# A two-layer hybrid attention block: five moves in the order of issue

## The chip, the core and the metric

The kernel runs on one core of one Trainium2 chip. The metric is the device time of one execution in microseconds, lower is better. A core has a matrix engine (TensorE, PE in the profile, with its weight loads as PEld), a vector engine (VectorE, DVE), an activation engine (ScalarE, ACT), a general engine (GpSimd, POOL) and a queue engine (SyncE, SP), which here issues nearly all DMAs. Each engine works its own list of instructions from first to last. TensorE's clock has two levels, 1.2 and 2.4 GHz; the profile calls the share that was granted PEclk, 1.00 for the higher.

## The reference

Two layers over 256 latent tokens and 256 context tokens of width 1024. Each layer computes, for both kinds of tokens (context only as far as the latents need it in the second layer):

```python
mod = silu_c @ lp["w_mod"] + lp["b_mod"]            # six vectors of 1024: shift, scale, gate, twice
h = modulate(x, lp["g_norm1"], sh1, sc1)            # RMSNorm, then scale and shift
proj = h @ lp["w_in"]
o_mla = blocked_attend(q_mla, k_mla, v_mla, MLA_QK ** -0.5)     # 8 heads
o_gqa = blocked_attend(q_gqa, k_gqa, v_gqa, GQA_DIM ** -0.5)    # 8 heads over 2 key heads
o_four = fourier_mix(proj[..., FOUR_START:GATE_START])          # 2-D DFT over 4 groups of 128 channels
y = (g_mla * (o_mla @ lp["w_br_mla"]) + g_gqa * (o_gqa @ lp["w_br_gqa"])
     + g_four * (o_four @ lp["w_four"]))            # g_* = sigmoid of gate columns of proj
x = x + gt1 * (y @ lp["w_o"])
u = conv3(modulate(x, lp["g_norm2"], sh2, sc2) @ lp["w_up"])
x = x + gt2 * ((silu(u[:D_FF]) * u[D_FF:]) @ lp["w_down"])      # D_FF = 2816
```

All of it is in float32.

## The kernel before

**Precision and weights.** Every large product is made of three matmuls of a reduced float32 type: each operand is split into a high part (a copy on ACT) and a low part (a subtraction on DVE), by `split` (L115), and `mm3` (L103) issues high by high (L104), high by low (L105) and low by high (L106). `wchunk` (L80) loads a chunk of a weight matrix in pieces of 1024 columns' worth (512 KB each, on SP), and splits each piece. The raw pieces, their high and their low parts have three buffers each (`RAWBUFS`, `WBUFS`).

**Who sets the order.** The program is traced in the order of the Python code. Tile then makes each engine's list with a simulated timeline: of the instructions that are ready in the simulation, the one traced earliest goes first, so a later piece of code can be drawn into a hole. `tc.issue_after(ins)` adds an edge: what a block traces on the engine of `ins` stands behind `ins` in that engine's list. It is no wait at run time. `after(mark)` (L111) does the same with an instruction noted in `marks`. `last_mm[0]` is the latest traced matmul of `mm3`.

**A layer** (`layer`, L445) works 512 tokens in layer 0 and 256 latent tokens (with 512 for keys and values) in layer 1. In order: the norm; keys and values of GQA (`kvg`, L500); GQA's queries in two chunks of 256 columns (`qg`, L519); the Fourier branch (`fo`, L596, with the DFT as matmuls from L610); GQA's heads, between which `fillers` put gate and branch products; then `latents`, `kv_tokens` and `q_tokens`, which make MLA's keys and queries; MLA's eight heads, after each of which an entry of `plan` (L897) is traced; the last branch; the output projection with `w_o` (L966 on); the second norm; the feed-forward.

**Gates and branches.** `merge` (L556) gives a gate function (`gG` for GQA, `gM` for MLA: 8 k x 2 x 3 = 48 matmuls and a tanh) and a branch function (`bG`, `bM`: 4 k x 2 x 3 = 24 matmuls, then a multiply on DVE and an addition into y on POOL). Their matmuls have 512 columns in layer 0 and 256 in layer 1.

**MLA's first heads.** `heads_kq(h)` (L905) transposes the keys and the queries of head h on TensorE and splits them. Head 0's is traced right behind `bG(0)`. The key tokens end with a multiply on POOL (L785), the query tokens with a rope on POOL (L495 to L498).

**The output projection.** Four chunks of 256 columns; each runs k = 0 to 7 over `ys`, the split y. The last two of the y come from the last branch product.

**Layer 1's start.** The last down projection of layer 0 ends in two halves of 256 tokens, and layer 1's norm of the latent half (`seq(0)`) is traced between them. The norm of the context half (`seq(1)`) is traced at the start of layer 1; `kvg` then takes the two latent token tiles first and the two context tiles after them.

**The sums.** The modulation vectors of layer 1 are made during layer 0's feed-forward. `mod_sums` (L277) makes, for each of five blocks of 1024 columns, eight steps: a load of 512 KB of `w_mod`, and one or two multiply-adds over it on DVE (L291 for the first k, L293 for the others); the eighth step ends with matmuls (L300), a copy and two transposes. `sums(n)` (L987) traces the next n steps: one behind each pair of columns j of the up projection, four behind the loads of each group of the down projection. The feed-forward runs in two halves of 12 and 10 of the 22 column blocks; a down group is one of four chunks of `w_down` over all k of its half.

## Time and profile before

| | before |
|---|---|
| median of 3 runs | 1407.85 us (1403.91 to 1409.02) |
| the profiled execution | 1404.45 us |
| its span, first to last instruction | 1402.7 us |
| TensorE busy | 1348.4 us (96%) |
| DVE busy | 945.7 us (67%) |
| ACT busy | 660.3 us (47%) |
| POOL busy | 337.5 us (24%) |
| mean granted TensorE clock | 0.982 |
| DMA moved | 197.40 MB, mean 141 GB/s |

The chain of work that ended last lies on TensorE for 86% of the span and on DVE for 7%. Busy times of matmuls overlap, since matmuls are pipelined, so the rate of TensorE is read from counts: instructions in a window of known length. A window's idle time is its length less the busy time.

### The profile page before, as it was taken

What the parts mean: (1) busy time and instruction counts of PE and PEld (TensorE: products, weight loads), DVE (VectorE), ACT (ScalarE), POOL (GpSimd) and SP (SyncE); (2) the same over time, 40 slices, a digit from 0 to 9 for tenths busy, and PEclk for the clock granted to TensorE, in tenths of its full rate; (3) what the DMA queues carried; (4) which work ended last, traced back from release to release, by engine and by line L of the source; (5) the groups of instructions that cost most, each with busy time, mean ns of one, the idle gap of its engine ahead of it and who ended that gap; (6) DMA issues with size and microseconds to landing.
All of it is one profiled execution on the core that took longest, in us unless ns stands there. A gap on an engine that the chain in (4) does not pass through costs nothing.

```text
span 1402.7 us, 22232 instructions
## 1 busy us (share of the span) xinstructions
PE 1348.4 (96%) x8381; PEld 1177.3 (84%) x8381; DVE 945.7 (67%) x1686; ACT 660.3 (47%) x1166; POOL 337.5 (24%) x399
## 2 busy tenths in 40 slices
PE   7999999999999997999999999999997999899998
PEld 4988888878888786887888888888987998899998
DVE  4575665666655669998635664578787766788853
ACT  4444554435554333444223443355664764566642
POOL 3212332374323411111100112122244432112200
PEclk9999999999999998999999999999998999999999
DMA  9733442143321736577632423354423345465663
GB/s 322 243 90 105 151 143 79 54 123 106 90 66 43 268 124 186 162 231 233 201 108 81 126 85 102 103 154 120 125 81 102 106 129 191 134 182 181 182 196 118
DMA packets 160437, 197.40 MB, mean 141 GB/s; under 512 B 7080, under 2 KB 144858, under 8 KB 160330
## 3 DMA queue, kind: packets, MB, share of 16 engines
q1 hardware_dynamic: 159328, 195.32, 45.2%
q0 software_dynamic: 864, 0.61, 0.4%
q8 instruction: 66, 1.08, 0.3%
q14 instruction: 41, 0.34, 0.1%
q10 hardware_dynamic: 138, 0.04, 0.0%
HBM read 191.76 MB, written 3.15 MB: 139 GB/s over the span
## 4 chain that ended last, share of the span: by engine, by line
PE 86%; DVE 7%; DMA 2%; issue 2%; POOL 1%; ACT 1%; SPq 0%; DVEq 0%; ACTq 0%; POOLq 0%
PE L0upp L106 5%; PE L0upp L104 5%; PE L0upp L105 5%; PE L1upp L104 3%; PE L1upp L105 3%; PE L1upp L106 3%; PE L0gp L106 3%; PE L0dp L104 3%; PE L0gp L105 3%; PE L0dp L105 3%; PE L0dp L106 3%; PE L0gp L104 3%; PE L1dp L106 1%; PE L1dp L105 1%; PE L1dp L104 1%
## 5 line engine op out<-in xcount | busy, mean ns | idle before, releaser
L105 PE MATMUL L0upp<-L0n_h,L0up_h 128*128 128x512 f32 (+1 forms) x384 | 144.8, 380 | 4.0 <-POOL L0n_h L373 2.4
L104 PE MATMUL L0upp<-L0n_h,L0up_h 128*128 128x512 f32 (+1 forms) x384 | 144.2, 379 | 2.6 <-ACT L0n_h L370 1.1
L106 PE MATMUL L0upp<-L0n_h,L0up_l 128*128 128x512 f32 (+1 forms) x384 | 142.7, 379 | 0.3 <-DVE L0up_l L124 0.3
L1031 POOL TENSOR_TENSOR L0sg<-L0sg,L0u 128x512 f32<-128x512 f32 x22 | 34.5, 1571 | 275.6 <-DVE L0u L1008 255.6
L104 PE MATMUL L1upp<-L1n_h,L1up_h 128*128 128x256 f32 x352 | 96.9, 287 | 1.1 <-ACT L1n_h L370 1.1
L106 PE MATMUL L1upp<-L1n_h,L1up_l 128*128 128x256 f32 x352 | 96.8, 285 | 0.0
L105 PE MATMUL L1upp<-L1n_h,L1up_h 128*128 128x256 f32 x352 | 96.3, 285 | 0.0
L105 PEld LDWEIGHTS L0upp<-L0n_h,L0up_h 128*128 128x128 f32 x384 | 74.0, 193 | 17.8 <-POOL L0n_h L373 2.6
L104 PEld LDWEIGHTS L0upp<-L0n_h,L0up_h 128*128 128x128 f32 x384 | 73.6, 193 | 16.5 <-ACT L0n_h L370 1.5
L106 PEld LDWEIGHTS L0upp<-L0n_h,L0up_l 128*128 128x128 f32 x384 | 73.7, 192 | 14.8 <-DVE L0up_l L124 1.1
L118 ACT CAST L0up_h<-L0up_w 128x1024 fp32r<-128x1024 f32 x44 | 46.4, 1054 | 76.3 <-PE L0upp L105 51.6
L124 DVE TENSOR_TENSOR L0up_l<-L0up_w,L0up_h 128x1024 fp32r<-128x1024 f32 x44 | 55.9, 1269 | 32.6 <-ACT L0up_h L118 32.3
L293 DVE SCALAR_TENSOR_TENSOR mod_acc<-mod_w,cpad,mod_acc 128x1024 f32<-128x1024 f32 x49 | 70.6, 1456 | 9.5 <-DMA mod_w<-in_w_mod_dram 9.5
L104 PE MATMUL L0gp<-L0n_h,L0g_h 128*128 128x512 f32 x192 | 76.6, 400 | 0.0
L105 PE MATMUL L0gp<-L0n_h,L0g_h 128*128 128x512 f32 x192 | 76.2, 397 | 0.0
L106 PE MATMUL L0gp<-L0n_h,L0g_l 128*128 128x512 f32 x192 | 75.7, 400 | 0.0
L104 PE MATMUL L0dp<-L0act,L0dn_h 128*128 128x512 f32 (+1 forms) x196 | 72.2, 368 | 0.0
L106 PE MATMUL L0dp<-L0act,L0dn_l 128*128 128x512 f32 (+1 forms) x196 | 72.1, 368 | 0.0
L105 PE MATMUL L0dp<-L0act,L0dn_h 128*128 128x512 f32 (+1 forms) x196 | 72.1, 368 | 0.0
L104 PEld LDWEIGHTS L1upp<-L1n_h,L1up_h 128*128 128x128 f32 x352 | 67.1, 195 | 1.8 <-ACT L1n_h L370 1.8
L106 PEld LDWEIGHTS L1upp<-L1n_h,L1up_l 128*128 128x128 f32 x352 | 67.2, 194 | 0.0
L124 DVE TENSOR_TENSOR L1up_l<-L1up_w,L1up_h 128x1024 fp32r<-128x1024 f32 x44 | 54.2, 1232 | 18.9 <-ACT L1up_h L118 17.5
(1564 smaller groups left out, 4279.2 us busy)
## 6 DMA issues: line engine op xcount, KB each, us to landing
mod_w<-in_w_mod_dram SPq DMA_DIRECT2D x96, 512.0 KB, 4.6
L0up_w<-in_w_up_dram SPq DMA_DIRECT2D x44, 512.0 KB, 3.6
L1up_w<-in_w_up_dram SPq DMA_DIRECT2D x44, 512.0 KB, 4.4
L0g_w<-in_w_in_dram SPq DMA_DIRECT2D x24, 512.0 KB, 3.7
L1g_w<-in_w_in_dram SPq DMA_DIRECT2D x24, 512.0 KB, 3.7
L0dn_w<-in_w_down_dram SPq DMA_DIRECT2D x20, 512.0 KB, 3.9
L1dn_w<-in_w_down_dram SPq DMA_DIRECT2D x16, 512.0 KB, 3.6
L0wo_w<-in_w_o_dram SPq DMA_DIRECT2D x8, 512.0 KB, 7.4
```

Source lines behind the costliest of these rows:

```text
L104: nc.tensor.matmul(ps, lh, rh, start=start, stop=False)
L105: nc.tensor.matmul(ps, lh, rl, start=False, stop=False)
L106: last_mm[0] = nc.tensor.matmul(ps, ll, rh, start=False, stop=stop).ins
L118: nc.scalar.copy(hi, src)
L124: nc.vector.tensor_sub(lo, src, f(hi))
L293: nc.vector.scalar_tensor_tensor(acc, raw, cv, acc, op0=ALU.mult, op1=ALU.add)
L1031: nc.gpsimd.tensor_mul(g[:, :TQ], g[:, :TQ], us[1][:, :TQ])
```

## The change

Five edits, all in the order of issue or the place of buffers; what is computed is the same.

- `sums`: each step is now traced under `after("split")` and `after("load")`, so its multiply-adds stand on DVE behind the latest traced low part of a split, and its load on SP behind the latest traced weight load. The eighth step gives back its closing matmuls as `add_up`; they wait in `late` for the next call of `sums`, which traces them behind the last matmul. A call `sums(0)` stands ahead of layer 1's first norm.
- Output projection: chunks 0 and 1 are loaded together; k = 0 to 5 of both run, then k = 6, 7 of both. Chunks 2 and 3 are as before.
- Layer 1's start: the first query chunk is traced between `kvg` of the latent tiles and `kvg` of the context tiles, with split tiles of its own (B0, B1, B2, D0) and in the `pt` banks.
- MLA: gate 1 (layer 0) or 2 (layer 1) of GQA is traced ahead of head 0's transposes, and these stand behind its last matmul on TensorE. In `plan` the gate is left out; in layer 1 the later entries move up by one and the last is empty.
- DFT: the loop over the four groups is outside the loop over the sequences.

In the diff below, the old places of the `kvg` loop and of its evacuation are left out; the loop itself is the one that stands there behind `q_chunk`.

```diff
-    def wchunk(W, k0, nk, c0, ncol, name):
+    def wchunk(W, k0, nk, c0, ncol, name, own=None):
...
-            hi = wpool.tile([P, WMAX], F32R, tag="whi", name=f"{name}_h{i}", bufs=WBUFS)
-            lo = wpool.tile([P, WMAX], F32R, tag="wlo", name=f"{name}_l{i}", bufs=WBUFS)
+            if own:
+                hi, lo = (S.tile([P, WMAX], F32R, tag=t, name=f"{name}_{x}{i}") for x, t in zip("hl", own[len(parts)]))
+            else:
+                hi = wpool.tile([P, WMAX], F32R, tag="whi", name=f"{name}_h{i}", bufs=WBUFS)
+                lo = wpool.tile([P, WMAX], F32R, tag="wlo", name=f"{name}_l{i}", bufs=WBUFS)
             split(raw[:, :n], hi[:, :n], lo[:, :n])
...
-        w.last = ins.ins
+        w.last = marks["load"] = ins.ins
...
         def low():
             if scale is None:
-                nc.vector.tensor_sub(lo, src, f(hi))
+                ins = nc.vector.tensor_sub(lo, src, f(hi))
             else:
-                nc.vector.scalar_tensor_tensor(lo, src, scale, f(hi), op0=ALU.mult, op1=ALU.subtract)
+                ins = nc.vector.scalar_tensor_tensor(lo, src, scale, f(hi), op0=ALU.mult, op1=ALU.subtract)
+            marks["split"] = ins.ins
...
-            if k < KD - 1:
-                return
+            return add_up if k == KD - 1 else None
+
+        def add_up():
             ps = pm(f"{name}_ps{blk}", "tk")
...
+        def q_chunk(c, banks, own=None):
+            w = wchunk(w_in, 0, KD, 928 + c * 256, 256, f"{n_}qg{c}", own)
             marks[f"qg{c}"] = w.last
             for tt in range(NTQ):
                 ts = slice(tt * P, (tt + 1) * P)
-                ps = pm(f"{n_}qg{tt}{c}", ("mm", "s")[tt % 2])
+                ps = pm(f"{n_}qg{tt}{c}", banks[tt % 2])
...
+        for tts in ((0, 1), (2, 3)) if l else (range(4),):
+            for k in range(KD):
+                wh, wl = w3(k, 0, 288)
...
+                        mm3(pss[tt][:, :288], hs[k][:, 0, ts], hs[k][:, 1, ts], wh, wl, k == 0, k == KD - 1)
+            if l and tts[0] == 0:
+                q_chunk(0, ("pt", "pt"), [("B0", "B1"), ("B2", "D0")])
...
+        for c in range(1 if l else 0, 2):
+            q_chunk(c, ("mm", "s"))
...
-        for s in range(NS):
-            for g in range(4):
+        for g in range(4):
+            for s in range(NS):
                 b, hf = (g, s) if NS == 2 else divmod(g, 2)
...
         if last:
-            plan = [[(bG, 1)], [(gG, 2)], [(bG, 2)], [(gG, 3)], [(bG, 3)], [(gM, 0)], [(gM, 1)], [(gM, 2)], [(gM, 3, "D4")]]
+            plan = [[(bG, 1)], [(bG, 2)], [(gG, 3)], [(bG, 3)], [(gM, 0)], [(gM, 1)], [(gM, 2)], [(gM, 3, "D4")], []]
         else:
-            plan = [[(gG, 1), (bG, 1)], [(gG, 2), (bG, 2)], [(gG, 3), (bG, 3)], [],
+            plan = [[(bG, 1)], [(gG, 2), (bG, 2)], [(gG, 3), (bG, 3)], [],
                     [(gM, 1, "X3")], [(gM, 2, "mraw")], [(gM, 3, "mraw")], [], [(gM, 0)]]
...
-        kq = heads_kq(0)
+        gG(2 if last else 1)
+        with tc.issue_after(last_mm[0]):
+            kq = heads_kq(0)
...
-        for mc in range(4):
+
+        wos, pos = [], []
+        for mc in range(2):
+            wos.append(wchunk(a["w_o"][l], 0, KD, mc * 256, 256, f"{n_}wo{mc}"))
+            pos.append([pm(f"{n_}o{mc}_{i}", ("mm", "s")[mc]) for i in range(2)])
+        for ks in (range(6), range(6, KD)):
+            for mc in range(2):
+                for k in ks:
+                    for i in range(2):
+                        wh, wl = wos[mc](k, i * P, P)
+                        mm3(pos[mc][i][:, :TQ], wh, wl, ys[k][:, 0, :TQ], ys[k][:, 1, :TQ], k == 0, k == KD - 1)
+                if ks[-1] == KD - 1:
+                    for i in range(2):
+                        residual(mc * 2 + i, pos[mc][i][:, :TQ], 16)
+        for mc in range(2, 4):
...
         def sums(n):
-            for step in mods["v"][:n]:
-                step()
+
+
+            todo, late[:] = late[:], []
+            for r in todo:
+                with tc.issue_after(last_mm[0]):
+                    r()
+            with after("split"), after("load"):
+                late.extend(r for r in [step() for step in mods["v"][:n]] if r)
             del mods["v"][:n]
+        late = []
...
                 elif mc == 3 and j0:
                     fm_halves(w, [0, P], jn, acts, lambda i, s_, ps: residual_half(mc * 2 + i, s_, ps, 40), f"{n_}dp{j0}{mc}",
-                              lambda: nxt.append(next_norm(xn)))
+                              lambda: (sums(0), nxt.append(next_norm(xn))))
```

## Rows read from the trace of the kernel before

**Rows 1.** The page, part 1: busy us, share of the span, instructions.

```profile
PE 1348.4 (96%) x8381; PEld 1177.3 (84%) x8381; DVE 945.7 (67%) x1686; ACT 660.3 (47%) x1166; POOL 337.5 (24%) x399
```

**Rows 2.** Windows at full stream: length, busy (count) by engine, PEclk, DMA share, GB/s.

```profile
700.00:725.00 25.00, 25.00 (x112) 20.71 (x111) 8.03 (x12) 5.13 (x5) 0.00 (x0) 1.00 0.34 106
...
1250.00:1275.00 25.00, 25.00 (x210) 25.00 (x210) 21.52 (x35) 16.38 (x26) 5.01 (x4) 1.00 0.60 182
```

**Rows 3.** Windows over the places that the edits name, same columns.

```profile
92.00:110.00 18.00, 15.39 (x94) 13.65 (x93) 12.91 (x24) 9.98 (x23) 1.59 (x2) 0.91 0.17 55
276.00:306.00 30.00, 26.95 (x124) 21.70 (x123) 25.49 (x39) 10.36 (x15) 20.36 (x17) 1.00 0.37 106
452.00:464.00 12.00, 8.83 (x39) 6.66 (x38) 12.00 (x13) 6.65 (x10) 10.20 (x6) 1.00 0.55 185
...
526.00:562.00 36.00, 27.65 (x168) 24.04 (x167) 34.41 (x45) 12.39 (x19) 5.43 (x3) 0.81 0.63 188
...
902.00:922.00 20.00, 16.96 (x112) 13.01 (x105) 17.11 (x55) 11.37 (x29) 3.26 (x5) 0.83 0.42 126
...
1068.00:1082.00 14.00, 7.91 (x35) 6.03 (x34) 6.51 (x12) 3.86 (x9) 5.19 (x8) 0.64 0.25 76
1140.00:1156.00 16.00, 16.00 (x135) 15.92 (x133) 9.27 (x14) 9.09 (x16) 3.19 (x5) 1.00 0.51 155
1163.00:1181.00 18.00, 14.59 (x103) 13.43 (x102) 14.12 (x21) 8.03 (x15) 5.14 (x3) 0.91 0.41 130
```

**Rows 4.** Waits of TensorE: who, for whom, us in total, times, longest.

```profile
PE L1kvg L104 <- ACT L1n_h L370: 2.9, 2, 1.8
PE mod_ps L300 <- DVE mod_acc L293: 2.8, 2, 2.3
...
PE L0m0tk L909 <- POOL L0ktok L785: 2.0, 3, 0.9
PE L0o L105 <- DVE L0yh L126: 2.0, 1, 2.0
```

**Rows 5.** Timeline of DVE, head of layer 0's feed-forward: start, us, what.

```profile
526.78 2.47 DVE L293 SCALAR_TENSOR_TENSOR mod_acc<-mod_w,cpad,mod_acc 128x1024 f32<-128x1024 f32 x2
529.17 0.48 DVE L369 SCALAR_TENSOR_TENSOR L0n_t<-L0x,L0A,L0n_rb 128x256 f32<-128x256 f32 x1
```

**Rows 6.** The line L293: durations min/median/max, first and last; its waits.

```profile
L293 DVE SCALAR_TENSOR_TENSOR mod_acc<-mod_w,cpad,mod_acc x49: 1268/1279/2311, 526.8 to 687.8; 128x1024 f32<-128x1024 f32 x49
...
  DMA mod_w<-in_w_mod_dram: 9.5, 7
```

**Rows 7.** Groups on DVE, 700 to 750 us: count, busy us, mean ns, idle before.

```profile
L956 DVE SCALAR_TENSOR_TENSOR L0x<-L0dp,modT,L0x 128x256 f32<-128x256 f32 x12 | 5.0, 478 | 8.0 <-PE L0dp L106 8.0
L124 DVE TENSOR_TENSOR L0dn_l<-L0dn_w,L0dn_h 128x1024 fp32r<-128x1024 f32 x4 | 4.9, 1220 | 8.4 <-ACT L0dn_h L118 8.4
```

**Rows 8.** Timeline of ACT, end of layer 0's DFT.

```profile
102.40 0.58 ACT L836 CAST L0KG<-L0gk 64x512 fp32r<-64x512 f32 x1
...
104.78 0.17 ACT L633 COPY L0z<-L0Zc 128x4 f32<-128x4 f32 x1
```

**Rows 9.** Timeline of POOL, head of MLA in layer 1.

```profile
1071.50 1.10 POOL L495 TENSOR_TENSOR L1qmr0b<-L1qtok,Bqm 128x128 f32<-128x128 f32 x1 [10.42 <-DVE L1qtok L814]
...
1074.58 0.46 POOL L495 TENSOR_TENSOR L1qmr1b<-L1qtok,Bqm 128x128 f32<-128x128 f32 x1
...
1076.21 0.72 POOL L498 TENSOR_TENSOR L1qtok<-L1qmr1a,L1qmr1b 128x256 f32<-128x256 f32 x1
```

**Rows 10.** Timeline of ACT, start of layer 1.

```profile
911.98 0.73 ACT L1124 CAST dft1d<-dft1r 128x256 fp32r<-128x256 f32 x2 [1.96 <-DMA dft1r<-in_dft_d_dram]
```

**Rows 11.** Timeline of DVE, start of layer 0's output projection.

```profile
456.64 4.43 DVE L124 TENSOR_TENSOR L0wo_l<-L0wo_w,L0wo_h 128x1024 fp32r<-128x1024 f32 x2
```

**Rows 12.** The DMA view: issues by tile, KB each, median us to landing.

```profile
mod_w<-in_w_mod_dram SPq DMA_DIRECT2D x96, 512.0 KB, 4.6
...
L0qg_w<-in_w_in_dram SPq DMA_DIRECT2D x4, 512.0 KB, 8.9
```

32 lines of the change are left out of this document (13 added, 19 removed).

## The prediction

> **What bounds the kernel now.** I read the page's busy table first: TensorE is busy 1348.4 of 1402.7 us, DVE 945.7 [rows 1]. So only two things can shorten the run: TensorE's idle time, 54 us, and stretches in which its clock stood at the lower of its two levels. Undisturbed, the stream takes 25/112 = 0.223 us for a matmul of 512 columns and 25/210 = 0.119 us for one of 256 [rows 2]; no edit touches that work. Next I cut the span into the places that the edits name, and read for each the idle time (length minus PE busy) and the lost clock (length times one minus PEclk) [rows 3]: the DFT of layer 0, 2.6 idle and 1.6 lost to the clock; head of MLA in layer 0, 3.05 and 0; start of the output projection of layer 0, 3.2 and 0; head of the feed-forward of layer 0, 8.35 and 6.8; start of layer 1, 3.0 and 3.4; head of MLA in layer 1, 6.1 and 5.0; output projection of layer 1, 3.4 and 1.6. Together 29.7 + 18.4 = 48.1 us. That is a ceiling: some of the slow clock lies on idle time and is counted twice. All else in the sum is how much of each place the edit reaches. Then the waits of TensorE tell who is late there [rows 4].
>
> **Part 1, the sums (L283 to L311, issued from `sums`).** In the head of the feed-forward the multiply-adds of layer 1's modulation sit between the steps of the norm: pairs of 2.47 us, each ahead of a norm step of 0.48 on DVE's queue, with TensorE waiting for the norm [rows 5]; then TensorE itself waits in `mod_ps` for the accumulator, 2.8 us in 2 waits [rows 4]. The 40 steps hold 56 sums (two rows in the first two blocks of eight steps, one in the other three); the 49 that accumulate ran from 527 to 688 us [rows 6]. The change puts each step behind the latest split on DVE and its load behind the latest weight load on SP, and the closing matmuls one call later behind the last matmul traced. So none can stand before the first two columns' splits: 12 sums fall to the first half's six column pairs, 26 to its four down groups, 5 to the second half's pairs, 13 to its down groups. The head loses its cause. The idle is 8.35; with all the clock it would be 15.2, but the two overlap in part. I take 11 gained, ends 6 and 14: the norm's own steps and weight splits may leave a short wait.
>
> What they cost where they go: a down group of layer 0's first half is 12 x 2 x 3 = 72 matmuls, 72 x 0.223 = 16.1 us. DVE has there 3 splits of 1.22 and 4 residuals of 0.48, 5.6 us [rows 7]; the heaviest groups add 8 sums of 1.28 [rows 6], 10.2. That is 15.8 of 16.1. It fits, barely, for two groups of four; the whole half needs 33 + 22 = 55 of 64 us. Queued behind each sum are the next group's weight splits, and behind a sum's load on SP the next weight loads. I take 1 us lost, ends 0 and 10.
>
> **Part 2, DFT by group.** TensorE waits for ACT's copy of the second bank's z, which stands behind four key copies of 0.58 on ACT's queue [rows 8]. With the group loop outside, the first bank is complete after a quarter of the 48 small matmuls instead of five eighths, so the splits and z run some 2 us earlier; but the first group now needs the fourth token tile at once. Ceiling 4.2; I take 3, ends 4.2 gained and 1 lost (that tile's split late). Layer 1 has one s, its order stays.
>
> **Part 3, a gate ahead of MLA's first transposes.** The gate's matmuls move forward and the transposes are put behind them on TensorE. In layer 0 it waits 2.0 us in three waits for POOL's keys [rows 4]; with 48 x 0.223 = 10.7 us of gate ahead these vanish. Queued behind the transposes are head 0's scores, for which only its own softmax waits; the gate's two loads on SP now pass the next branch's, which is used later. I take 2 of 3.05, ends 3 gained and 1 lost. In layer 1 the gate gives 48 x 0.119 = 5.7 us of cover for a place with 6.1 idle and 5.0 of clock. The last wait there is for POOL's rope, which ended at 1076.9 [rows 9]; the gate adds two weight splits to DVE's queue ahead of that chain, 2 x 1.22 by the same shape of [rows 7], so I take 6, ends 11 gained and 1 lost. One pair of rows bears on the lower end: the first rope step took POOL 1.10 us, the same step of the next tile 0.46 [rows 9]. The Trainium skill ("SBUF — State Buffer", section "SBUF: two separate sides") says that a DVE operation with two SBUF inputs and a GpSimd one lock each other out for a whole instruction, as splits of weights would do to the rope. The rows agree with it; if three of the eight rope steps met a split, that would be 3 x 0.64 = 1.9 us later, and by that rule the gain would be nearer 4 than 6.
>
> The gate is taken from the plan of the heads, whose last entry in layer 1 becomes empty: the last head has one gate behind it instead of two. TensorE was busy all 16 us of that stretch [rows 3], and 5.7 us of it go. I take 1 lost, ends 0 and 4, since the last head's own chain is not all covered by what is left.
>
> **Part 4, first queries between keys.** At layer 1's start TensorE waits twice: 2.9 us in all, the longest 1.8 [rows 4]: for a norm step on ACT that stood behind a copy waiting 1.96 for the DFT table's DMA [rows 10], and for the first step of the context half. The chunk's 48 x 0.119 = 5.7 us cover the second wait and let the clock stay up; the first stands ahead of the chunk. Its own tiles let its splits run early, but 2 x 1.22 us more of DVE then compete with the norm, and its two banks are shared with the modulation bursts. On SP its loads pass nothing new: they already stood first after those of `kvg`, and the DFT table's follow them as before. Ceiling 6.4; I take 4, ends 6.4 gained and 1 lost.
>
> **Part 5, output projection in pairs.** It holds back k = 6, 7 of two chunks. But in layer 0 the wait is for the first yh low half, standing behind two weight splits of 4.43 us [rows 4, 11]; it is the only wait of `L0o` for a yh, and it is not at k = 6. So I take 1 for both layers, ends 8 gained (the whole of both places, order falling well) and 2 lost (four parts in three weight buffers).
>
> **Sum**: 11 - 1 + 3 + 2 + 6 - 1 + 4 + 1 = 25 us gained. The profiled execution took 1404.45 us; 25 less is 1379.5. The median of three runs is 3.4 above it, so on that scale 1407.85 - 25 = 1382.9, say 1383. All good ends together give 14 + 0 + 4.2 + 3 + 11 + 0 + 6.4 + 8 = 46.6, all bad ones 6 - 10 - 1 - 1 - 1 - 4 - 1 - 2 = -14; they will not fall together.
>
> **Rivals.** A: the chains, not the cover, set both heads. The extra splits push the rope chain of layer 1 back and the tail loses its gate; then only the sums and the DFT count, 11 - 1 + 3 = 13: 1395. For it: the rope chain ends the last wait, and one of its steps was already stretched to 1.10 us [rows 9]. Against: DVE was idle for half of that stretch, 6.5 of 14 us busy [rows 3], so it has room for two splits.
>
> B, the slower side: the down groups wait for the sums' loads. Two load buffers and four steps a group give a step (load + sums)/2. At the median 4.6 us [rows 12] it is (4.6 + 2.56)/2 = 3.6, 14.3 a group: under 16.1. At 8.9, what a 512 KB load took where loads crowd [rows 12], it is 5.7, 22.9 a group: 6.8 over in four groups; the second half, 60 matmuls and 13.4 us a group, one sum of 1.28 a step, has 20.4, 7.0 over in three. That is 48 lost, 1383 + 48 = 1431. It decides against the change from about 7.2 us a load, where 4 x (2 x (7.2 + 2.56) - 16.1) + 3 x (2 x (7.2 + 1.28) - 13.4) = 24 us are lost, about all that the edits gain. For it: sums already waited 9.5 us for loads [rows 6]. Against: DMA moved 106 GB/s in that stretch [rows 2], the sums add 16 x 0.52 MB in 64 us, 131 more, and the median load is two thirds of the breaking point.
>
> C: the edits hardly show, since the instruction order comes from a simulated schedule that need not place the work as the text suggests, and new waits appear as the old ones go: 1407 give or take 6.
>
> **Chances.** Forecast 0.61 (1360 to 1392), A 0.17, C 0.12, B 0.10. A difference under 0.5% (7 us) can't be told from none in this kernel. Faster by over 0.5% means below 1400.8: forecast and A, 0.78; the same, C, 0.12; slower, B, 0.10. The range 1367 to 1406 holds most of the forecast, A and half of C: about 0.81.
>
> **What would show it.** Part 1: no L293 before 550 us, the head's PE busy near its length at clock 1.00, sums spread to the end of layer 0; wrong if PE goes idle in the down groups. Part 2: no wait in L0Zc. Part 3: no wait for L1m2tk, `gp` ahead of L1m0tk, and TensorE full behind the last head. Part 4: `L1qg` between the two `L1kvg` runs. Part 5: little. I am wrong if the idle leaves these places but the span does not shrink by it.

## The result, and the profile after

The changed kernel took 1387.35 us, the median of four runs (1384.54 to 1390.6), against 1408.43 (1403.91 to 1409.15) for the kernel before on the same chip: ratio 0.9858, 95% interval 0.9827 to 0.9889. So it is faster by 21 us, 1.4%, beyond the 0.5% that this kernel can resolve; 1383 was forecast, within 1367 to 1406. The profiled execution took 1388.23 us with a span of 1386.4.

The page of the changed kernel, part 1 (busy us, share of the span, instructions) and the clock line of part 2 (tenths of full clock in 40 slices):

```profile
PE 1339.8 (97%) x8381; PEld 1171.6 (85%) x8381; DVE 949.8 (69%) x1686; ACT 660.7 (48%) x1166; POOL 334.4 (24%) x399
...
PEclk8999999999999999999999999999999999999999
```

Beside [rows 1]: the instruction counts are the same, and the other engines are as busy as before, to 1%. TensorE's busy time fell by 8.6 us, because at the higher clock the same matmuls are shorter (its mean granted clock rose from 0.982 to 0.988, and 0.006 of the span is 8.3 us); the rest of the 16.3 us of span is idle time that went.

The places of [rows 3] again, moved along with the work: length, busy us of PE, PEld, DVE, ACT and POOL (count), PEclk, DMA share, GB/s. They are the DFT of layer 0, the head of MLA in layer 0, the start of its output projection, the head of its feed-forward, the start of layer 1, the head of MLA there, its last head, its output projection:

```profile
94.00:112.00 18.00, 15.39 (x95) 13.75 (x94) 13.15 (x24) 10.22 (x23) 1.58 (x2) 0.91 0.17 57
278.00:308.00 30.00, 27.84 (x130) 22.83 (x129) 25.95 (x39) 10.36 (x15) 20.13 (x17) 1.00 0.38 106
455.00:467.00 12.00, 8.79 (x36) 6.63 (x35) 12.00 (x12) 6.25 (x9) 9.80 (x6) 0.94 0.62 193
529.00:565.00 36.00, 36.00 (x218) 32.31 (x218) 25.67 (x34) 17.68 (x24) 4.35 (x4) 1.00 0.40 129
892.00:912.00 20.00, 14.63 (x79) 13.12 (x80) 15.49 (x43) 10.43 (x25) 1.77 (x2) 0.83 0.59 179
1059.00:1073.00 14.00, 11.73 (x86) 10.29 (x85) 9.10 (x13) 7.29 (x12) 6.24 (x8) 1.00 0.46 130
1131.00:1147.00 16.00, 14.65 (x121) 14.36 (x120) 8.22 (x14) 7.62 (x16) 5.10 (x7) 1.00 0.55 176
1150.00:1168.00 18.00, 16.50 (x130) 15.60 (x129) 15.64 (x22) 8.44 (x15) 5.95 (x3) 1.00 0.56 174
```

The fourth line is the great success: 27.65 of 36 busy at clock 0.81 before, 36.00 of 36 at 1.00 now, and 218 matmuls where there were 168. The first line is as before to the hundredth: 15.39 of 18.00 at 0.91. The fifth is worse: 14.63 of 20 busy, where it was 16.96. The sixth looks far better, 11.73 of 14 at full clock against 7.91 at 0.64, and is a trap, as the next table shows.

A window says how full a place is, not how long it takes. So I cut the span at fixed matmuls: a boundary is the start of the first, or the end of the last, matmul that writes a tile, read from TensorE's list of each trace. A column is one profiled execution. Lengths in us:

| from | to | before | after | sums only | no query move | no gate | no pairs | early query load | keys behind | wo behind | three |
|---|---|---|---|---|---|---|---|---|---|---|---|
| span's start | first L0fp | 71.02 | 73.26 | 73.88 | 73.48 | 71.23 | 71.65 | 73.83 | 73.96 | 71.99 | 73.86 |
| first L0fp | first L0uq | 198.14 | 198.09 | 198.14 | 198.15 | 198.15 | 196.56 | 198.17 | 194.43 | 197.90 | 194.42 |
| first L0uq | last L0m7o | 177.88 | 178.29 | 177.84 | 178.28 | 177.88 | 178.29 | 178.32 | 177.94 | 178.20 | 178.19 |
| last L0m7o | first L0upp | 68.80 | 68.78 | 68.80 | 68.72 | 67.18 | 68.70 | 68.74 | 68.76 | 65.30 | 65.27 |
| first L0upp | last L0dp | 386.01 | 372.53 | 372.58 | 372.71 | 372.56 | 372.48 | 372.81 | 372.57 | 372.37 | 372.97 |
| last L0dp | first L1fp | 35.91 | 38.27 | 36.63 | 36.11 | 39.55 | 37.94 | 32.62 | 38.72 | 38.05 | 34.23 |
| first L1fp | first L1ukv | 86.39 | 85.90 | 86.39 | 86.40 | 85.89 | 85.89 | 85.87 | 85.90 | 85.88 | 85.89 |
| first L1ukv | first L1m0s | 55.21 | 55.38 | 55.01 | 55.39 | 55.26 | 56.92 | 55.39 | 55.52 | 55.37 | 55.39 |
| first L1m0s | last L1m7s | 61.55 | 61.27 | 61.19 | 61.30 | 60.80 | 61.27 | 61.28 | 61.30 | 61.27 | 61.30 |
| last L1m7s | first L1o | 25.76 | 21.62 | 25.76 | 21.62 | 25.76 | 21.64 | 21.62 | 21.63 | 21.62 | 21.62 |
| first L1o | last L1o | 29.33 | 26.07 | 29.32 | 27.37 | 29.04 | 30.38 | 27.36 | 26.07 | 26.07 | 26.06 |
| last L1o | last matmul | 202.85 | 203.16 | 202.72 | 203.28 | 202.61 | 203.75 | 203.76 | 203.18 | 203.09 | 202.42 |

From before to after: 13.5 gained in the feed-forward, 0.4 lost in MLA of layer 0, 2.4 lost at the start of layer 1, nothing at the head of MLA there (55.21, 55.38), 4.1 gained behind its last score and 3.3 in its output projection. The start-up, which no edit touches, was 2.2 longer (it goes from 71.0 to 75.2 in the fourteen traces); all rows together make 16.2. Lengths of stages that two kernels share repeat to 0.1 to 0.6 us, unless the clock fell in one of them. The exception is the start of layer 1: with the query chunk as in the changed kernel it took 37.8 to 39.6 us in nine traces, without the chunk 35.9 to 36.6 in three. The times of one kernel spread over 1 to 9 us. So small effects are judged by this table, and the medians say at most whether they arrive.

What TensorE waits for in the changed kernel, from 80 us on (who, for whom, us in total, times, longest):

```profile
PE L1kvg L108 <- ACT L1n_h L376: 2.6, 2, 1.4
PE L0Zc L108 <- ACT L0z L644: 2.6, 1, 2.6
...
PE L0o L109 <- DVE L0yh L130: 2.0, 1, 2.0
PE L0bp L110 <- DVE L0b_l L128: 1.8, 2, 1.2
PE L1kvg L110 <- POOL L1n_h L379: 1.5, 1, 1.5
PE L1bp L108 <- ACT L1m5om L701: 1.4, 1, 1.4
PE L1o L109 <- DVE L1yh L130: 1.3, 2, 1.0
```

Against [rows 4]: the waits for the accumulators (but for 0.3 us) and for POOL's keys went, those of `L0Zc`, `L1kvg` and `L0o` are still there, and new ones stand in `L0bp` (two of its three; one of 1.2 us was there before), in `L1bp` and in `L0m0pt`.

### The profile page after: what moved, and what is told of

Its sections match the earlier page's. It is cut to its first block, busy times and chain, and to the rows that moved or that the text cites. A ratio compares the mean times of both kernels' runs of the same rounds, so it can differ in the third digit from the quotient of the medians.

```text
span 1386.4 us, 22211 instructions
## 1 busy us (share of the span) xinstructions
PE 1339.8 (97%) x8381; PEld 1171.6 (85%) x8381; DVE 949.8 (69%) x1686; ACT 660.7 (48%) x1166; POOL 334.4 (24%) x399
## 4 chain that ended last, share of the span: by engine, by line
PE 86%; DVE 6%; issue 3%; DMA 2%; POOL 2%; ACT 1%; SPq 0%; DVEq 0%; ACTq 0%; POOLq 0%
PE L0upp L109 6%; PE L0upp L108 6%; PE L0upp L110 6%; PE L1upp L108 3%; PE L1upp L109 3%; PE L1upp L110 3%; PE L0gp L109 3%; PE L0gp L110 3%; PE L0gp L108 3%; PE L0dp L108 2%; PE L0dp L109 2%; PE L0dp L110 2%; PE L1gp L110 2%; PE L1dp L110 2%; PE L1dp L109 2%
## 5 line engine op out<-in xcount | busy, mean ns | idle before, releaser
L108 PE MATMUL L0upp<-L0n_h,L0up_h 128*128 128x512 f32 (+1 forms) x384 | 141.5, 372 | 1.1 <-ACT L0n_h L376 1.1
L109 PE MATMUL L0upp<-L0n_h,L0up_h 128*128 128x512 f32 (+1 forms) x384 | 142.5, 373 | 0.0
L110 PE MATMUL L0upp<-L0n_h,L0up_l 128*128 128x512 f32 (+1 forms) x384 | 139.1, 371 | 0.0
L1065 POOL TENSOR_TENSOR L0sg<-L0sg,L0u 128x512 f32<-128x512 f32 x22 | 29.6, 1343 | 273.9 <-DVE L0u L1042 273.9
L108 PEld LDWEIGHTS L0upp<-L0n_h,L0up_h 128*128 128x128 f32 x384 | 71.9, 188 | 14.4 <-ACT L0n_h L376 1.5
L109 PEld LDWEIGHTS L0upp<-L0n_h,L0up_h 128*128 128x128 f32 x384 | 72.2, 188 | 13.0 <-DVE L0n_t L375 0.4
L128 DVE TENSOR_TENSOR L0up_l<-L0up_w,L0up_h 128x1024 fp32r<-128x1024 f32 x44 | 59.2, 1347 | 34.2 <-ACT L0up_h L122 33.7
L298 DVE SCALAR_TENSOR_TENSOR mod_acc<-mod_w,cpad,mod_acc 128x1024 f32<-128x1024 f32 x49 | 62.9, 1308 | 18.6 <-DMA mod_w<-in_w_mod_dram 18.4
L110 PE MATMUL L0gp<-L0n_h,L0g_l 128*128 128x512 f32 x192 | 75.2, 398 | 0.0
L108 PEld LDWEIGHTS L1upp<-L1n_h,L1up_h 128*128 128x128 f32 x352 | 67.3, 196 | 1.8 <-ACT L1n_h L376 1.8
L128 DVE TENSOR_TENSOR L1up_l<-L1up_w,L1up_h 128x1024 fp32r<-128x1024 f32 x44 | 54.5, 1238 | 19.2 <-ACT L1up_h L122 17.8
```

The source lines that it names most:

```text
L108: nc.tensor.matmul(ps, lh, rh, start=start, stop=False)
L109: nc.tensor.matmul(ps, lh, rl, start=False, stop=False)
L110: last_mm[0] = nc.tensor.matmul(ps, ll, rh, start=False, stop=stop).ins
L128: ins = nc.vector.tensor_sub(lo, src, f(hi))
L298: nc.vector.scalar_tensor_tensor(acc, raw, cv, acc, op0=ALU.mult, op1=ALU.add)
L1065: nc.gpsimd.tensor_mul(g[:, :TQ], g[:, :TQ], us[1][:, :TQ])
```

## The experiments

All run on one core; each has a median of four to seven runs, and its ratio is to the kernel before on the same chip, whose medians went from 1406.99 to 1408.43 us. A difference from the changed kernel is one between two such medians, from different chips for the most part. By the intervals of the ratios, the changed kernel (0.9827 to 0.9889) is told apart from those with the sums alone, without the sums and without the gate, and from the one with three moves; for the others the medians alone decide nothing, and the table of stages carries the argument.

### The sums alone, and all but the sums

The first kernel is the one before with this part of the change; the second is the changed kernel without it:

```diff
-            for step in mods["v"][:n]:
-                step()
+            todo, late[:] = late[:], []
+            for r in todo:
+                with tc.issue_after(last_mm[0]):
+                    r()
+            with after("split"), after("load"):
+                late.extend(r for r in [step() for step in mods["v"][:n]] if r)
```

> The kernel before with the sums edit alone (the 49 products of layer 0's feed-forward issued behind a split's low part and behind a load, each vector's transposes and last sum put off to the next call). The theory: the sums carry nearly all of the gain, because the changed kernel's first projection of the feed-forward ends 16.9 us earlier relative to its start while its down projection and the start of layer 1 give back about 6. Expected: 13 to 17 us under the kernel before, ratio 0.988 to 0.991, with no TensorE gaps beyond 1 us per 25 us in the up projection. The rival: the gain of that stage needs the other edits (for example the paired output projection that sets when the first splits are made), then it is under 6 us, ratio above 0.996.

> The changed kernel with the sums edit undone alone. The theory: the other four edits together are worth 5 to 8 us (the wait for the first tail transposes and the paired chunks at the end of layer 1, less what the start of layer 1 lost), so the time is 1400 to 1404, ratio 0.994 to 0.997, and the gaps of 13 to 14 us in the up projection are back. The rival: edits overlap in what they hide, and without the sums the others are worth nothing or more than 10 us: ratio over 0.999 or under 0.992.

Alone the edit gives 1395.09 us (ratio 0.9912, 0.9889 to 0.9934), 13.1 under the kernel before. The changed kernel without it takes 1401.01 (0.9945, 0.9925 to 0.9964), 13.7 over the changed kernel. The two agree, so the sums are two thirds of the gain and the other four edits are worth about 7. Windows over the feed-forward of layer 0 up to the last down product, of the kernel before and of the one with the sums alone:

```profile
515.85:901.86 386.01, 377.37 (x1842) 314.02 (x1846) 267.36 (x351) 141.40 (x194) 48.06 (x36) 0.98 0.48 147
```

```profile
518.65:891.24 372.59, 371.56 (x1842) 309.88 (x1846) 268.35 (x351) 142.11 (x194) 44.92 (x36) 1.00 0.48 152
```

The same 1842 matmuls; idle falls from 8.64 to 1.03, and the clock rises from 0.98 to 1.00 (the 36 us at 0.81 of [rows 3] lie here: 6.8 us that were lost). That is 7.6 + 6.8, less 1.0 in which both fell together, for the 13.4 us by which the stretch is shorter.

### The closing matmuls at once

The sums edit has two halves: the sums behind splits and loads, and each vector's closing put off by a call. This kernel is the changed one with the first half alone:

```diff
-                late.extend(r for r in [step() for step in mods["v"][:n]] if r)
+                closing = [r for r in [step() for step in mods["v"][:n]] if r]
+            for r in closing:
+                r()
```

> The changed kernel where the sums are still issued behind a split and a load, but the closing matmuls of each vector at once instead of one call later. The theory: the gain of the sums is that they no longer stand in front of the norm's steps and in front of the loads; the later closing is worth at most what TensorE waited there before, 2.8 us, and by program order only some twenty products move; expected 0 to 2 us slower than the changed kernel, 1387 to 1389.5. The rival: the late closing is what spares TensorE the waits for the accumulators, which came twice at over 1 us each with four closings still to come, then 4 us or more slower, over 1391.

1387.65 us (0.9857, 0.9841 to 0.9874), and the feed-forward takes 372.62 us against 372.53. The putting off is worth nothing that can be measured; the gain is the place of the sums.

### Without the query chunk between the keys

```diff
-            if l and tts[0] == 0:
-                q_chunk(0, ("pt", "pt"), [("B0", "B1"), ("B2", "D0")])
...
-        for c in range(1 if l else 0, 2):
+        for c in range(2):
```

> The changed kernel without layer 1's query chunk between its two key groups (both query chunks again behind the keys). Theory after seeing the trace of the changed kernel: the chunk's second half loads late, its cast waits 3.81 us at the head of ScalarE's queue and its low part 2.50 us on VectorE, in front of the norm steps that TensorE waits for; without the chunk the start of layer 1 is shorter by 2 to 3 us, time 1384 to 1385.5, ratio 0.983 to 0.985. The rival, which was the prediction's: the chunk covers gaps, and without it TensorE's waits between the first keys and the first queries grow by 2 to 6 us: time 1389 to 1393, ratio 0.987 to 0.990.

1386.54 us (0.9848, 0.9826 to 0.987): by time no difference. By the table the start of layer 1 is 2.2 us shorter without the edit (38.27 to 36.11), 0.5 longer just behind it, and 1.3 was given back in the output projection, where the clock fell this time. So the chunk did not help, but whether the cause is its late load is not shown by leaving it out. In the trace of the changed kernel ScalarE and TensorE stand like this (start, us; in brackets the idle time before and who ended it):

```profile
899.23 1.04 ACT L122 CAST L1qg_h<-L1qg_w 128x1024 fp32r<-128x1024 f32 x1 [3.81 <-DMA L1qg_w<-in_w_in_dram]
900.18 1.30 ACT L376 ACTIVATE L1n_h<-L1n_t,modT 128x256 fp32r<-128x256 f32 x3
```

```profile
900.73 0.40 PE L108 MATMUL L1kvg<-L1kvg_h,L1n_h 128*128 128x288 f32 x1 [1.38 <-ACT L1n_h L376]
...
903.06 0.85 PE L110 MATMUL L1kvg<-L1kvg_h,L1n_h 128*128 128x288 f32 x2 [1.53 <-POOL L1n_h L379]
```

The cast of the chunk's second half waits 3.81 us for its load at the head of ScalarE's queue; the norm steps that TensorE waits for stand behind it.

### The query chunk with buffers of its own for the load

In the changed kernel the two loads were issued at 888.59 and 894.13 us. SyncE's list there, and the split that gave back the second raw buffer:

```profile
888.59 0.37 SPq L90 DMA_DIRECT2D L1qg_w<-in_w_in_dram  x1
891.58 2.46 SPq L473 DMA_DIRECT2D L1xk<-L0x  x4
894.13 1.23 SPq L90 DMA_DIRECT2D L1qg_w<-in_w_in_dram  x2
```

```profile
890.38 1.06 DVE L128 TENSOR_TENSOR L1kvg_l<-L1kvg_w,L1kvg_h 128x864 fp32r<-128x864 f32 x1 [0.83 <-ACT L1kvg_h L122]
```

The first load came when its raw buffer was free: the split that read it ended at 888.56. The second buffer was free at 891.44, but four loads of `L1xk` stood ahead of the chunk's second load on SyncE, until 894.04. The kernel of this run lets the chunk load into the two buffers of the modulation weights, which the sums have left by then:

```diff
-            raw = wpool.tile([P, WMAX], F32, tag="raw", name=f"{name}_w{i}", bufs=RAWBUFS)
+            raw = wpool.tile([P, WMAX], F32, tag="mraw" if own else "raw", name=f"{name}_w{i}", bufs=2 if own else RAWBUFS)
```

> The changed kernel with layer 1's first query chunk loaded into two buffers of its own (those that the modulation weights of the feed-forward leave free), so that its loads needn't wait until the down projection gives back weight buffers (issued at 888.59 and 894.13 us in the changed kernel). The theory: the late second load is what held ScalarE (3.81 us) and VectorE (2.50 us) ahead of the norm steps; with early loads TensorE's gaps between 897 and 912 us fall from 4.2 us to under 2 and the lower clock there goes, 3 to 5 us faster than the changed kernel, 1382.5 to 1384.5. The rival: the norm's own chain of steps on VectorE and ScalarE is the limit, whatever stands in front of it, then the gaps only move and the time is within 1 us of 1387.

1383.81 us (0.983, 0.9808 to 0.9851), 3.5 under the changed kernel by medians. The start of layer 1 falls from 38.27 to 32.62 us, and that is 3.5 under the kernel without the chunk too. SyncE in this kernel, and TensorE's waits from 890 to 930 us:

```profile
879.20 0.38 SPq L90 DMA_DIRECT2D L1qg_w<-in_w_in_dram  x1
882.26 0.37 SPq L90 DMA_DIRECT2D L1qg_w<-in_w_in_dram  x1
```

```profile
PE L1kvg L108 <- ACT L1n_h L376: 1.4, 1, 1.4
PE L1n_ss L360 <- ACT L1n_sq L348: 0.5, 1, 0.5
```

The loads are 9 and 12 us earlier, both ahead of those of `L1xk` now, and the wait for POOL is gone. The DFT table's loads moved forward with them (the first to 882.72 from 895.48 us): its first two casts on ScalarE, which stood between the norm steps at 901.8 and 902.8, the second after a wait of 0.6, are done by 892 here. So with its loads early the chunk gains in this trace nearly what was forecast. The run took away the wait for a buffer, the place behind `L1xk` and the late table together, and doesn't tell what each cost.

### Without the gate ahead of MLA's first transposes

```diff
-        gG(2 if last else 1)
-        with tc.issue_after(last_mm[0]):
-            kq = heads_kq(0)
+        kq = heads_kq(0)
```

with `plan` as it was before.

> The changed kernel with latent attention's first transposes ahead of the gate again, in both layers, and the gate chunks back in their old places. The theory: in layer 1 the gain was at the other end, where the gate chunk moved behind the last head covers 4.05 us before the output projection, while in layer 0 the move lost 0.4 us and at the head of layer 1's attention nothing came; expected 3 to 4 us slower than the changed kernel, time 1390 to 1391.5, ratio 0.987 to 0.989. The rival: the covered gap at the head of attention was worth its 6 us and only looked unchanged because something else came late; then about 8 us slower, ratio over 0.990; or the gate does nothing at all and the time stays at 1387.

1395.32 us (0.9905, 0.9884 to 0.9927), 8 slower than the changed kernel by medians. The profiled execution, the fastest of its six (1391.53), is only 3.3 slower by its span, 5.3 without the start-up, which was 2 us shorter here. The table says where: 25.76 instead of 21.62 behind the last score, 29.04 instead of 26.07 in the output projection; in MLA of layer 0 it is 0.4 faster without the gate; and at the head of MLA in layer 1 it takes 55.26 instead of 55.38. So the size in the rival's sentence came by the medians, but not its reason: the head of attention gave nothing. Of the step from the trace's 5.3 to the median's 8, 1.6 lies in the output projection of layer 0: TensorE waited its 2.0 us there as ever, but in this execution the clock did not fall behind it (67.18 against 68.78 us). The rest isn't settled; the five other runs have a lower mean clock (0.982 or 0.983, against 0.986 in the profiled one). The windows over that head, of the changed kernel and of this one:

```profile
1015.12:1070.51 55.39, 49.61 (x329) 44.57 (x327) 46.82 (x94) 33.50 (x68) 30.10 (x34) 1.00 0.37 104
```

```profile
1012.43:1067.69 55.26, 45.61 (x288) 40.50 (x287) 45.62 (x94) 31.24 (x65) 29.05 (x34) 0.95 0.36 103
```

41 more matmul records in the same length, so the gate's 48 ran in time that was idle or slow, and the place got no shorter. It is the tail, where they were taken away, that did.

### The rope of layer 1's queries on VectorE, without the gate

This asks what holds the head of MLA in layer 1 at 55 us:

```diff
-                rope_apply(nc.gpsimd, qtok[tt][:, :, 64:96], qtok[tt][:, :, 64:96], "qm", tt, H, 32, f"{n_}qmr{tt}")
+                rope_apply(nc.vector if last else nc.gpsimd, qtok[tt][:, :, 64:96], qtok[tt][:, :, 64:96], "qm", tt, H, 32, f"{n_}qmr{tt}")
```

> The changed kernel without the gate edit (as in the run without it, 1395.3 us, whose trace took 55.26 us from layer 1's first key and value product of latent attention to head 0's first score), and with the eight rope steps of layer 1's queries on VectorE instead of GpSimd. It asks what sets the head of latent attention in layer 1. The theory: the rope chain on GpSimd, 5.4 us from 1059.82 to 1065.25, is what the first score waits for, whatever TensorE is given meanwhile; with steps of 0.2 to 0.35 us on VectorE it takes 2 to 3 us, and the stretch of 55.26 us falls to 52 to 53. The rival: the query transposes wait for something else as late (VectorE's queue with the weight splits of the gate chunks), then the stretch stays at 55 or over.

1391.39 us (0.9893, 0.9877 to 0.991) against 1395.32, and the head takes 53.56 instead of 55.26 us. GpSimd's rope in the kernel without the gate (first and last step), and VectorE's here:

```profile
1059.82 1.10 POOL L501 TENSOR_TENSOR L1qmr0b<-L1qtok,Bqm 128x128 f32<-128x128 f32 x1 [10.46 <-DVE L1qtok L825]
...
1064.53 0.72 POOL L504 TENSOR_TENSOR L1qtok<-L1qmr1a,L1qmr1b 128x256 f32<-128x256 f32 x1
```

```profile
1061.59 0.74 DVE L130 SCALAR_TENSOR_TENSOR L1m1k<-L1m1tk,gk,L1m1k 96x512 fp32r<-96x512 f32 x1
1062.25 0.28 DVE L501 TENSOR_TENSOR L1qmr0b<-L1qtok,Bqm 128x128 f32<-128x128 f32 x1
...
1064.42 0.42 DVE L504 TENSOR_TENSOR L1qtok<-L1qmr1a,L1qmr1b 128x256 f32<-128x256 f32 x1
```

The chain takes 2.6 us instead of 5.4, and 1.1 of these 2.8 are lost since it starts later in the stage, behind the second tile's multiply and the low part of head 1's keys; 1.7 remain, and by 1.7 the first score comes earlier. So the rope sets that head in the kernel without the gate, if with a smaller step than the 2 to 3 us expected. The rest of the 3.9 between the medians isn't from here; 1.4 of it lies in the output projection in the trace (29.04 and 27.60), where the clock fell for less time.

### Without the pairs

The changed kernel with the four chunks of the output projection one after the other:

```diff
-        wos, pos = [], []
-        for mc in range(2):
...
-        for mc in range(2, 4):
+        for mc in range(4):
```

> The changed kernel with the output projection's chunks one after the other again, the gate chunk still behind the last head. In the run without the gate edit the paired projection saved 0.7 us of TensorE gaps at layer 1's output projection (3.28 before, 2.54 there) but met 6.8 us at the lower clock instead of 3.4, so the pairs alone gave nothing there. The theory: the pairs and the gate chunk work together, the gaps come back to about 5 us and the lower clock with them, and the time is 2 to 4 us above the changed kernel, 1389.5 to 1391.5, ratio 0.987 to 0.989. The rival: the whole gain of 7.3 us around layer 1's output projection came from the gate chunk's cover, and without pairs the time stays within 1 us of 1387.4, ratio 0.985 to 0.986.

1392.12 us (0.9888, 0.9868 to 0.9907), 4.8 over the changed kernel, a little more than the theory's range. In the trace the output projection took 4.3 us longer (30.38 against 26.07). The span was only 2.8 longer: the DFT was 1.5 shorter, since the clock did not fall there, and the head of MLA in layer 1 1.5 longer, since it did. With the run without the gate this makes a table of four, windows over layer 1's output projection: before, pairs without gate, gate without pairs, both:

```profile
1166.68:1196.00 29.32, 25.91 (x199) 24.62 (x201) 18.17 (x25) 12.18 (x19) 9.40 (x7) 0.94 0.52 158
```

```profile
1154.26:1183.30 29.04, 26.50 (x199) 26.01 (x201) 18.54 (x25) 11.61 (x19) 9.43 (x7) 0.88 0.53 159
```

```profile
1151.34:1181.72 30.38, 27.62 (x200) 26.21 (x202) 18.40 (x27) 12.94 (x21) 9.41 (x7) 0.89 0.49 155
```

```profile
1153.40:1179.47 26.07, 24.57 (x200) 23.53 (x202) 18.76 (x27) 12.36 (x21) 9.46 (x7) 1.00 0.59 178
```

Idle is 3.41, 2.54, 2.76 and 1.50: each edit takes 0.65 to 0.9 us off, both 1.9. The clock does the rest: it lost 1.8, 3.5, 3.3 and 0 us (length times one minus PEclk). With either edit alone the place is no better than before; with both it is 3.3 shorter. Of that, 1.3 is not secured: in three other kernels with both edits the clock fell there all the same, to 0.94 in each, and they took 27.28 to 27.37.

### The DFT in its old order

```diff
-        for g in range(4):
-            for s in range(NS):
+        for s in range(NS):
+            for g in range(4):
```

> The changed kernel with the first DFT step again in the order sequence by sequence. In program order ScalarE's and VectorE's instructions come out the same, and on TensorE only nine products of layer 0's step move. The theory: no difference, time 1386 to 1389, ratio 0.9845 to 0.987, the 2.61 us gap after the first DFT still there and of the same size. The rival, which was the prediction's: the group order is worth 3 us, then 1390 to 1391, ratio over 0.987, and the gap is over 4 us long.

1387.64 us (0.9855, 0.9835 to 0.9876), the same as the changed kernel, and its window has the same 15.38 of 18.00:

```profile
94.00:112.00 18.00, 15.38 (x95) 13.74 (x93) 13.55 (x25) 10.34 (x23) 1.59 (x2) 0.91 0.19 59
```

### The key copies behind the DFT's

```diff
-            nc.scalar.copy(z3[:, :, 0:P + 1:P], zc[:, :, 0:P + 1:P])
+            marks["z"] = nc.scalar.copy(z3[:, :, 0:P + 1:P], zc[:, :, 0:P + 1:P]).ins
...
+            with after("z", l == 0):
+                nc.scalar.copy(KG[v][64 * v:64 * v + 64, 0, :], src)
+                nc.scalar.copy(KG[v][64 - 64 * v:128 - 64 * v, 0, :], src)
```

> The changed kernel with one thing moved: the four copies of the grouped keys (4 x 0.58 us on ScalarE) are issued behind the last small copy of the DFT's results. In the changed kernel they stand at 104.64 to 106.99 us in front of the copies that free the banks for the last two DFT products, and TensorE waits 2.61 us and then runs at the lower clock for 3.4 us. The theory: the wait is the place of these copies in ScalarE's queue, so the gap falls under 1 us and the lower clock goes: 3 to 4 us faster than the changed kernel, 1383 to 1384.5. The rivals: VectorE's chain of sums and splits (0.41 to 0.69 us each) takes the place of the copies, then the gap shrinks by under 1 us; or the grouped attention starts later because the keys come later, and the gain is lost there.

1385.01 us (0.9841, 0.9821 to 0.9861), 2.3 under the changed kernel; the stretch from L0fp to L0uq falls from 198.09 to 194.43. ScalarE in the changed kernel, then the window of this one:

```profile
104.64 0.58 ACT L847 CAST L0KG<-L0gk 64x512 fp32r<-64x512 f32 x1
...
106.41 0.58 ACT L848 CAST L0KG<-L0gk 64x512 fp32r<-64x512 f32 x1
107.01 0.17 ACT L644 COPY L0z<-L0Zc 128x4 f32<-128x4 f32 x1
```

```profile
94.00:112.00 18.00, 17.47 (x109) 15.38 (x108) 12.94 (x25) 10.31 (x23) 0.00 (x0) 1.00 0.19 59
```

Busy 17.47 of 18 at full clock, where it was 15.39 at 0.91. The queue order on ScalarE was nearly all of that wait; 0.2 us of it is left.

### The output weight's low parts behind the first yh

```diff
-            wos.append(wchunk(a["w_o"][l], 0, KD, mc * 256, 256, f"{n_}wo{mc}"))
+            wos.append(wchunk(a["w_o"][l], 0, KD, mc * 256, 256, f"{n_}wo{mc}", behind=() if l else [(None, yl[3]), (yl[5], yl[7])][mc]))
```

`behind` names, for each piece, the low part of a yh (`yl`) behind which its own split is issued.

> The changed kernel with one thing moved, in layer 0: the low part of the second piece of the first output weight chunk is issued behind the low part of yh 3 instead of ahead of yh 0, and those of the second chunk behind yh 5 and yh 7. In every kernel so far the two weight low parts take VectorE 4.43 us together, ahead of the first yh low part, while TensorE waits 2.02 us in the output projection and then runs 3.4 us at the lower clock. The theory, which is the prediction's reading of that wait: the queue order on VectorE is what ends last, so the 2.02 us wait goes and mostly the lower clock with it, 2 to 4 us faster than the changed kernel, 1383.5 to 1385.5. The rival: GpSimd's sums of y, which end late, set the pace, so that another wait of the same size comes for yh 1 to 3, and the time is within 1 us of 1387.

1386.55 us (0.9844, 0.9827 to 0.9862) is no measurable difference by time; its runs went from 1382.71, the profiled one, to 1387.03. By the table the stretch falls from 68.78 to 65.30, and the wait of `L0o` is gone. So the wait was there for that reason, and with it went 1.5 us of lost clock; by medians the gain shows only in the next kernel.

### Three of the moves at once

The early query load, the key copies behind the DFT's and the output weight's low parts behind yh, with the three diffs above.

> The changed kernel with three of the moves at once: the early query load, the grouped key copies behind the DFT's, and the output weight's low parts behind yh. Alone the first two gave 3.5 and 2.3 us by their medians (5.4 and 3.4 by the place in the trace). The theory: they lie in three places that share nothing, so their gains add up, 6 to 10 us with the third: 1377.5 to 1381.5, ratio 0.979 to 0.981. The rival: what one place gains is lost at the next wait for a load, since every place comes earlier against the same transfers; then 1382 to 1384.

1376.8 us (0.9781, 0.9761 to 0.98), 10.5 under the changed kernel and the fastest of all. Three stretches changed: 3.67 (DFT), 3.51 (output projection of layer 0) and 4.04 (start of layer 1), 11.2 together. The last was 5.65 alone. Its waits from 880 to 920 us:

```profile
PE mod_ps L260 <- DMA mod_w<-in_w_mod_dram: 1.1, 1, 1.1
PE L1kvg L109 <- ACT L1n_h L377: 1.1, 1, 1.1
PE L1n_ss L361 <- ACT L1n_sq L349: 0.5, 1, 0.5
```

A new wait for a modulation load has come, 1.1 us, so the rival is right in a small part: beside the kernel with the early load alone the stage begins 7.2 us earlier (884.72 against 891.88), and that load was issued only 5.6 earlier (897.42 against 902.99).

## Why the prediction was right, and where its steps were not

The time came within 4.4 us of the forecast by medians. In the profiled execution, where the sum was made, it came 8.7 short: 1379.5 against 1388.23, of which 2.2 is start-up. That the total came so near is in part luck: two steps below gave 5.8 us more than was forecast, and four gave 12.9 less. The steps one by one, in us gained:

| step | forecast | measured in the trace |
|---|---|---|
| sums, head and new place | 11 - 1 | 13.5, as 14.6 - 1.1 |
| DFT by group | 3 | 0 |
| gate, MLA of layer 0 | 2 | -0.4 |
| gate, head of MLA of layer 1, and tail | 6 - 1 | -0.2 + 4.1 |
| first queries between keys | 4 | -2.4 |
| pairs | 1 | 3.3, with the gate |

**Part 1 was right**, and a size was off: the head gave more than 11, since idle and slow clock overlapped less than assumed, by 1.0 us. The sums ran from 573 to 880 us, as the changed kernel's line shows beside [rows 6]:

```profile
L298 DVE SCALAR_TENSOR_TENSOR mod_acc<-mod_w,cpad,mod_acc x49: 1274/1280/1764, 573.1 to 879.5; 128x1024 f32<-128x1024 f32 x49
...
  DMA mod_w<-in_w_mod_dram: 18.4, 12
...
  PE mod_ps L306: 0.3, 1
```

They waited 18.4 us for their loads, twice as long as before. TensorE waited 0.3 us for them, and 0.8 once for the last weight split of the down projection, which stood behind two sums and four residual steps on DVE: the new place cost 1.1 us at most, about the 1 that was forecast. That answers rival B: the 40 loads took 4.5 us at the median and 4.9 at most, well under its breaking point of 7.2, and of DVE's waits no more than this 1.1 us reached TensorE there.

**Part 2 failed at "the splits and z run some 2 us earlier".** The row was read rightly: the key copies on ACT were the wait, as the kernel with the copies behind shows. But the edit doesn't touch them. The scheduler had already mixed the two sequences, so only a few products moved on TensorE, and ScalarE's and VectorE's lists stayed the same. The cause had been named and the edit credited with a cure that it doesn't contain.

**Part 3, layer 0, failed at the next branch's chunk, "which is used later".** The waits for POOL's keys and queries (2.0 and 1.1 us) went, but the gate's two loads and splits stand ahead of the branch's, and TensorE now waits for the branch's splits, for one of the query weights, and for head 0's softmax, 3.4 us in all. The cover came as forecast; its price, put at 1 of the 3.05 us, came to 3.4. In the nine traces of the other kernels with this gate the stage took 177.94 to 178.32 us, 0.1 to 0.4 more than before. The waits from the first query products to the end of MLA:

```profile
PE L0m0pt L672 <- POOL L0m0p L669: 1.3, 2, 0.9
PE L0bp L108 <- ACT L0b_h L122: 0.8, 1, 0.8
PE L0uq L109 <- DVE L0uq_l L128: 0.7, 1, 0.7
PE L0bp L110 <- DVE L0b_l L128: 0.6, 1, 0.6
```

**Part 3, layer 1, had nearly the right sum with the gain and the loss in the wrong places.** It failed where it counted cover as gain, for a place "with 6.1 idle and 5.0 of clock". There a window can deceive: idle of 6.1 became 2.3 and the clock returned to 1.00, and the first score came no earlier. Rival A's chain does set the head without the gate, as the run with the rope on VectorE shows, and what is put into a wait for a chain doesn't make the chain end sooner. In the changed kernel it ended 52.3 us into the stage, 52.8 without the gate. The gate's last product ended 0.1 us behind it, and TensorE waits for the rope no more. The query transposes came 1.6 us after that product, behind the key transposes and eight products of GQA's last head:

```profile
1066.69 0.74 POOL L504 TENSOR_TENSOR L1qtok<-L1qmr1a,L1qmr1b 128x256 f32<-128x256 f32 x1
```

```profile
1069.14 0.39 PE L925 MATMUL L1m0tq<-ident,L1qtok 128*96 128x128 f32 x2
```

So the gate took up the wait and then stood ahead of head 0 itself; whether the chain or TensorE's own list sets the head in the changed kernel no run separates. What was gained is the 5.7 us of matmuls that left the tail, less a new wait of 1.35 for the last heads' result (`L1bp`, under the tile name `L1m5om`): 4.1, but for 0.2. The forecast booked a loss there, and so did rival A. The rope row of [rows 9] was the right evidence. The Trainium skill ("SBUF — State Buffer", section "SBUF: two separate sides") says that DVE with two SBUF inputs and GpSimd shut each other out for whole instructions. The changed kernel agrees: a rope step took 1.43 us beside a weight split of 1.49, where the same step of the next tile took 0.46.

**Part 4 failed at "Its own tiles let its splits run early".** The tiles of its own are for the split parts. The loads still went through the three raw buffers, which came free late, and the second load stood behind four of `L1xk` on SP besides; that "its loads pass nothing new" there was true and no help. So the chunk's cast, traced ahead of the context norm, held up what it should have bridged. With early loads, which bring the DFT table early too, the edit gives 3.5 us against the kernel without it in one trace, near the 4 that was forecast, and 1.9 (36.11 to 34.23) in the kernel with three moves. How much of it is the cover alone is not shown.

**Part 5 was read rightly in layer 0** (68.80 and 68.78: nothing, for the reason given, as the kernel with the low parts behind yh shows) **and too low in layer 1**, where 1.9 us of idle and the clock's 1.8 went, though only with the gate behind the last head: alone the pairs gave 0.3 us (29.33 to 29.04).

Rival C, that nothing would show, is excluded by the ratio's interval.

## What to carry to other kernels

Where a chain sets the length of a hole, work that fills it shortens the run at the place that it leaves and not at the hole: read which chain ends last there before crediting the hole. When an edit moves a load's consumer forward, look for the buffer that the load needs and for what stands ahead of it in the queue, because a cast that waits for its load at the head of its engine's list holds all that stands behind it (3.81 us here). And compare stages between fixed instructions: a window's fill can rise from 57% to 84% with no gain at all.

## What the runs showed of the hardware

The same wait need not cost the same. The 2.61 us gap of the DFT was there in the changed kernel and in the one without pairs, with the same work around it; the window of the changed kernel is the first of the section on the result, 15.39 busy at 0.91, and this is the same 18 us in the kernel without pairs:

```profile
92.40:110.40 18.00, 15.38 (x101) 13.82 (x100) 13.14 (x24) 10.22 (x23) 1.59 (x2) 1.00 0.17 55
```

In the first the granted clock was at 1.2 GHz for a part of the time, in the second it stayed at 2.4, and the stretch from L0fp to L0uq took 198.09 and 196.56 us. The kernel with the closings at once also kept the clock there (196.57). Of the fourteen traces twelve have this gap, of 2.61 or 2.62 us; behind it the clock fell in ten and stayed in these two. Twelve have the wait of 2.0 us in the output projection of layer 0; there the clock fell in eleven, and stayed in the kernel without the gate (67.18 us against 68.78). So of a gap's price, idle and clock, the second part was met in some executions and not in others. Here it was 1.5 us on a gap of 2.61, and 1.6 on one of 2.0. Why it was spared in these three is not shown.
